# Summing the squares of the latent tokens on TensorE, and forming modulation columns one token tile later

## The chip, the cores and the metric

The kernel runs on one core of one Trainium2 chip. A core has five engines, each with its own instruction stream: TensorE (matrix products; PE in the profile, and PEld for its weight loads), VectorE (DVE), ScalarE (ACT), GpSimd (POOL) and SyncE (SP), which here only issues DMAs. They meet through semaphores alone. The metric is device time in microseconds (us), the median over several runs.

## The reference

Two layers of a transformer backbone on 512 latent tokens of width 1024, with 256 context tokens beside them. Each layer is `h += g1 * mixer(norm(h)); h += g2 * swiglu(norm(h))`; layer 0's mixer is a differential attention of 8 heads over latent and context tokens, layer 1's a short gated convolution. What bears on the change is the very first step, the modulated input of layer 0:

```python
mod = (silu(c) @ ada_w[i] + ada_b[i])                    # six vectors of 1024
sh1, sc1, g1, sh2, sc2, g2 = split(mod, 6)
a  = rmsnorm(x,   norm1[i]) * (1.0 + sc1)  + sh1         # latent tokens
ac = rmsnorm(ctx, norm1[i]) * (1.0 + csc1) + csh1        # context tokens
q, k, v = split(a @ w_qkv, ...)                          # and the same for ac
```

`rmsnorm` needs, for each token, the sum of its 1024 squares.

## The kernel before

Features lie on partitions, tokens along the free dimension. The 1024 features are 8 feature tiles (`KT`), the 512 latent tokens 4 token tiles (`LT`), the context tokens 2 more. Float32 products are made exact by splitting each operand in a high and a low part (`hi_w` and `lo_w` for weights, `aTh`/`aCh` and `aTl` for tokens) and adding three products. A plain float32 matmul, such as those of the statistics, leaves two records in the trace (two passes), so that 4 issued matmuls stand as x8.

The start of the program, all within the first 60 us, goes so. TensorE first runs 37 warm-up matmuls (`N_WARM`) on a tile of ones. `x_stats(LAT)` squares each of the 8 feature tiles of x on ScalarE (L268) and adds them up on VectorE (L270) in `ss`; then `stats` lets TensorE sum `ss` over the partitions, 4 matmuls with the data as stationary operand and 2 columns of ones as moving operand. VectorE scales the sums (`var_x`, L244), GpSimd takes the power -1/2 (`rs_x`, L247), VectorE makes diagonal matrices of the results (`dg_x`, L251), TensorE spreads them over all partitions (`x_bcast`) and ScalarE copies them to `bcs` (L276).

The modulation of a feature tile k takes three steps. `mod_dot(k)` multiplies the conditioning vectors with a 1 MB tile `ad` of the adaLN weights on TensorE, and ScalarE copies the result to `pas` (L311). `mod_cols(k)` turns it into columns by two small matmuls, and VectorE forms the shift (`mod`, L318) and the gain (`Gc`, L320). `mod_apply(k, i)` scales x on VectorE (L326), adds the shift and rounds to `aTh` on ScalarE (L327), and forms the rest `aTl` on VectorE (L328).

The loop over k then projects the first head: for each feature tile, three matmuls for each of the 4 latent token tiles into four PSUM banks, with the context tokens three steps behind. `mod_dot` runs two tiles ahead (`AHEAD`), and `mod_cols` of that tile ends the step. Weights of the first two heads come in units that a DMA loads (`raw_w`), ScalarE casts to `hi_w` (L180), and VectorE or GpSimd completes with `lo_w` (L181).

What sets the order: TensorE's stream is pinned to program order (`te.pin`, class `InOrder`, whose line 98 all its instructions bear). The streams of the other engines are ordered by the framework's scheduler when the program is built, and each engine then works its stream in order. Buffers come free by pool: the tag `sq` has 2 buffers, `ad` 4, `raw` 5, `pas` 2.

Of the kernel before, what the change touches and what calls it, by code (L numbers as in the profile page):

```python
# [14 lines left out]
# The order of issue in the attention. A head takes 24 positions, each with a quarter of the projections of  # L15
# one token tile of the next head (head 7: of one feature tile of the output projection); what else is issued,
# and at which position of its head, is listed here.
#   scores 0, scores 1, transpose 0, scores 2, transpose 1, scores 3, transpose 2, P V of tiles 0-1, transpose 3, P V of tiles 2-3
# [3 lines left out]
#   transposes of k tiles 2-3, q, k tiles 4-5 (head 0: k tiles 0-1, 2-3, q, k tiles 4-5)  # L22
TK = (2, 0, 4)
TK_OF = {0: (9, 9, 8, 10), 1: (0, 2, 4), 7: (3, 0, 3)}
#   transposes of k tiles 0-1 of the next head
TK_NEXT = 16
TK_NEXT_OF = {0: 12, 6: 15}
#   the weights of the head after the next, by feature tiles
W_AT = (16, 19, 22, 23, 23, 24, 26, 27)
W_AT_OF = {0: (11, 11, 15, 22, 22, 22, 25, 26)}  # L30
#   positions from the squares of a token tile to its rotation
LAG = 1
LAG_OF = {1: 0}
#   head 6: scale of the first six heads' outputs, its products, their exact parts
# [3 lines left out]
# halves of adaLN tiles per token tile of each head, per pair of gate and up tiles, per down tile  # L38
ADA_HEAD = (0, 2, 1, 1, 1, 1, 1, 1)
ADA_GATE, ADA_DOWN = 3, 3  # L40
# tile of the output projection before which the weights of the last two heads are staged
W67_AT = 6
# token tiles whose squares the activation engine also sums
ACC_TILES = (0, 1, 2, 3, 4)
# second parts of staged weights: 0 on the vector engine, 1 on the GpSimd engine
# [6 lines left out]
# the first head's projections: at which feature tile the second head's weights are staged, how many tiles the  # L52
# context lags behind the latent tokens, where its statistics and their broadcast come
W1_AT = (1, 2, 5, 5, 5, 8, 10, 10)
CTX_LAG, CTX_STATS, CTX_BCAST = 3, 1, 2
AHEAD = 2
N_WARM = 37
RAW_BUFS = 5
# pieces of the second half of the tokens after which the next norm's statistics and its products come
TURN = {8: (4, 7), 2: (1, 3)}  # L60
# feature tiles whose squares GpSimd sums for the norm after the attention
# [16 lines left out]
# columns of the packed parameters  # L78
# [9 lines left out]
class InOrder:  # L88
    """an engine; while pin is set its instructions are issued in program order"""
# [16 lines left out]
def kernel(  # L106
# [43 lines left out]
    mods = const.tile([P, 2, 6, KT], F32, name="mods")      # sh1 sc1 g1 sh2 sc2 g2  # L150
    part = const.tile([P, 2, 2, 6, KT], F32, name="part")   # halves of the dot products
    mod0 = const.tile([P, 2, 2, KT], F32, name="mod0")      # layer 0, latent and context: sh1 sc1
    Gc = const.tile([P, 5, KT], F32, name="Gc")             # norm gains times (1 + scale)
# [9 lines left out]
    # staging of the attention weights and the attention output: right stack  # L163
# [22 lines left out]
    def ada_half(i, half, pool, tag, bufs):  # L186
        """one half of the dot products of a tile of 128 columns of ada_w with silu(c)"""
        l, s, j = ada_list[i]
        raw = pool.tile([P, 512], F32, name=f"ada_{i}_{half}", tag=tag, bufs=bufs)
        nc.sync.dma_start(out=raw, in_=adaR[i, :, half * 512:(half + 1) * 512])  # L190
        ve.scalar_tensor_tensor(out=raw, in0=raw, scalar=1.0, in1=scrow[:, half * 512:(half + 1) * 512], op0=ALU.mult, op1=ALU.mult,  # L191
                                accum_out=part[:, half, l, s, j:j + 1])
# [10 lines left out]
    # =====================================================================  # L203
    # layer 0: modulated input, differential attention
    # =====================================================================
# [23 lines left out]
    # the tensor engine's clock rises while the first loads are under way  # L229
# [3 lines left out]
    # silu of the conditioning vectors  # L233
# [4 lines left out]
    def stats(sums, ntile, ps_stat, pool, nm):  # L238
        """rstd of the tokens from the columns of the partial sums, as diagonal matrices"""
        for t in range(ntile):  # L240
            for i, x in enumerate(sums):
                te.matmul(out=ps_stat[:, 2 * t:2 * t + 2], lhsT=x[:, t * P:(t + 1) * P], rhs=ones[:, 0:2], start=(i == 0), stop=(i == len(sums) - 1))
        var = pool.tile([P, 4], F32, name=f"var_{nm}", tag="var", bufs=1)
# [11 lines left out]
    def bcast(dgs, bc):  # L255
        """bc[t][:, q] = rstd of token q of tile t, the same on all partitions"""
# [3 lines left out]
    # 1 / rms of x and ctx, on all partitions  # L260
# [3 lines left out]
    def x_stats(s):  # L264
# [6 lines left out]
        return stats([ss[:, s]], n, pqkv0[5][:, SEQ - 16:], s0, f"x{n}")  # L271

# [27 lines left out]
    def mod_dot(k):  # L300
        """products of the conditioning vectors with the shift and scale columns of one feature tile"""
# [11 lines left out]
    def mod_cols(k):  # L313
        """shift and gain of one feature tile as columns, for the latent and the context tokens"""
# [7 lines left out]
    def mod_apply(k, i):  # L322
        """a = x rstd G + sh in two exact parts"""
# [11 lines left out]
    dgs = x_stats(LAT)  # L335
# [4 lines left out]
    for k in range(1, AHEAD):  # L340
        mod_dot(k)
        mod_cols(k)
    for k in range(KT + CTX_LAG):
# [5 lines left out]
        if k < KT:  # L349
            for t in range(LT):  # L350
                qkv_mm(pqkv0[t], t, k, W0[k])
        if j < KT:
            mod_dot(j)
        if k + 1 < KT:
# [9 lines left out]
        if j < KT:  # L364
            mod_cols(j)
# [6 lines left out]
    # gains of q and k folded into the rotary tables (q also takes 1 / sqrt(head dim))  # L372
# [9 lines left out]
    # lam = exp(q1 k1) - exp(q2 k2) + lam_init  # L382
# [30 lines left out]
    def qkv_post1(o, t, ps):  # L413
        """sums of squares of q and k of one token tile; v in two parts"""
# [21 lines left out]
    def qkv_post2(o, t, ps, st):  # L436
        """normalise and rotate q and k of one token tile"""
# [52 lines left out]
    def scores(o, t):  # L490
        """softmax of both maps for one tile of queries, combined: a = p0 - lam p1"""
# [58 lines left out]
    def o_rstd(b):  # L550
        """1 / sqrt(mean + eps) of the heads so far; 0 where the sum is beyond float32's range"""
# [12 lines left out]
    def o_apply(k):  # L564
        """o rstd subln (1 - lam_init), in place; rstd comes broadcast from DRAM"""
# [33 lines left out]
    def fill_qkv(nxt, W, t):  # L599
        """projections of one token tile of the next head, in quarters"""  # L600
# [14 lines left out]
    def fill_wo(n):  # L615
        """heads 0-5 of one feature tile of the output projection, in quarters"""
# [18 lines left out]
    def events(o, base):  # L635
        """what the attention of a head does, and from which position"""
# [75 lines left out]
    # =====================================================================  # L712
    # the rest: residual stream h (features on partitions), FFN and convolution
    # =====================================================================
# [21 lines left out]
    def residual(n, ps, gcol, nm, s=FULL):  # L736
        """h += gate * y for one feature tile; its squares go into the next norm's sum"""
# [17 lines left out]
    class Norm:  # L755
        """a = h rstd G + sh in two exact parts, by halves of the tokens"""
# [23 lines left out]
    def turn(last, norm):  # L780
        """the last products of a projection, by halves of the tokens, with the next norm's first half between them"""
# [14 lines left out]
    def group(U, norm, nm):  # L796
        """the first four units after a norm, the contraction outermost, by halves of the tokens"""
# [288 lines left out]
```

## Time and profile before

| | |
|---|---|
| time, median of 3 runs | 1342.76 us (1341.63 to 1345.31) |
| span of the profiled execution | 1343.2 us |
| TensorE busy | 1309.2 us (97%) |
| VectorE busy | 809.6 us (60%) |
| ScalarE busy | 503.9 us (38%) |
| GpSimd busy | 184.9 us (14%) |
| mean granted TensorE clock | 0.991 of full speed |

The profiled execution has no time of its own but its span, from the first to the last instruction; it lies 0.5 us above the median and inside the three runs. Busy shares are means over stages with different limits, so the start of the program is read by itself. A granted clock of 1.00 is 2.4 GHz and 0.50 is 1.2 GHz.

### The profile page before, as it was taken

The page shows a single profiled execution, that of the slowest core. Times are in us where ns is not written, and L with a number is a line of the kernel's source. Part 1 is how long each engine was busy: PE and PEld are TensorE (multiplying, and loading weights), DVE is VectorE, ACT ScalarE, POOL GpSimd, SP SyncE. Part 2 cuts the span into 40 slices and gives each one's busy share as a digit, 9 for nine tenths or more (in the row PEclk, how much of TensorE's full clock was granted, in tenths as well). Part 3 has the DMA queues.
Part 4 walks back from the last instruction along what each step waited for, and adds up shares of the span by engine and source line. Part 5 has one row for each costly group of instructions (what it writes and reads, how often), then busy time and mean ns, then how long its engine had stood idle before and what let it go on. Part 6 is the DMA issues. An engine that isn't in the chain of part 4 may idle for free.

```text
span 1343.2 us, 18899 instructions
## 1 busy us (share of the span) xinstructions
PE 1309.2 (97%) x7021; PEld 1130.8 (84%) x7021; DVE 809.6 (60%) x1598; ACT 503.9 (38%) x1125; POOL 184.9 (14%) x239
## 2 busy tenths in 40 slices
PE   8999999999999999899999999999999999999999
PEld 7889988998789888688888898888898888888887
DVE  5889888988968666665653366444664333333331
ACT  4677666776655321122221333222342212222120
POOL 0544444543302000000000020000100000000000
PEclk9999999999998999899999999999999999999999
DMA  9413333214333756677642333313323223322231
GB/s 350 160 41 112 94 95 90 71 59 146 106 118 103 224 197 196 198 241 224 203 134 67 110 109 109 97 55 96 118 72 121 81 72 109 125 94 85 70 105 40
DMA packets 72284, 164.59 MB, mean 123 GB/s; under 512 B 7784, under 2 KB 23424, under 8 KB 71168
## 3 DMA queue, kind: packets, MB, share of 16 engines
q1 hardware_dynamic: 72192, 163.38, 38.6%
q8 instruction: 55, 0.90, 0.3%
q14 instruction: 37, 0.30, 0.1%
HBM read 161.24 MB, written 2.11 MB: 122 GB/s over the span
## 4 chain that ended last, share of the span: by engine, by line
PE 74%; DVE 10%; DMA 8%; issue 3%; POOL 2%; ACT 2%; SPq 0%; POOLq 0%; DVEq 0%; ACTq 0%
PE pg L98 25%; PE pd L98 18%; PE pi L98 8%; PE pq L98 7%; DMA ada<-in_adaR_dram 6%; PE py L98 3%; PE s L98 3%; PE pw L98 3%; DVE ada L191 2%; PE pf_in L98 2%; PE pf_gu L98 2%; PE pv L98 1%; DMA xk<-in_xT_dram 1%; POOL st L432 1%; DMA raw_w<-in_wqkv_dram 1%
## 5 line engine op out<-in xcount | busy, mean ns | idle before, releaser
L727 ACT CAST sh_gu<-sr_gu 128x1024 fp32r<-128x1024 f32 x88 | 92.3, 1052 | 276.1 <-PE pg L98 147.9
L191 DVE SCALAR_TENSOR_TENSOR ada<-ada,scrow 128x512 f32<-128x512 f32 x160 | 110.6, 702 | 85.5 <-DMA ada<-in_adaR_dram 85.1
L728 DVE TENSOR_TENSOR sl_gu<-sr_gu,sh_gu 128x1024 fp32r<-128x1024 f32 x85 | 105.8, 1247 | 72.4 <-ACT sh_gu L727 65.3
L98 PE MATMUL pg<-xl_n0b,sh_gu 128*128 128x512 f32 x320 | 124.6, 389 | 0.0
L98 PE MATMUL pg<-xh_n0b,sh_gu 128*128 128x512 f32 x320 | 124.6, 389 | 0.0
L98 PE MATMUL pg<-xh_n1b,sh_gu 128*128 128x512 f32 x320 | 124.6, 389 | 0.0
L98 PE MATMUL pg<-xl_n1b,sh_gu 128*128 128x512 f32 x320 | 124.5, 389 | 0.0
L98 PE MATMUL pg<-xh_n1b,sl_gu 128*128 128x512 f32 x320 | 124.5, 389 | 0.0
L98 PE MATMUL pg<-xh_n0b,sl_gu 128*128 128x512 f32 x320 | 124.5, 389 | 0.0
L98 PE MATMUL pq<-hi_w,aTl 128*128 128x384 f32 (+1 forms) x336 | 108.5, 323 | 0.0
L98 PE MATMUL pq<-hi_w,aTh 128*128 128x384 f32 x224 | 77.3, 345 | 2.5 <-DVE qn L443 2.5
L839 DVE TENSOR_TENSOR sl<-sl,pg 128x512 f32<-128x512 f32 x40 | 27.4, 686 | 85.7 <-PE pg L98 85.7
L98 PE MATMUL pq<-lo_w,aTh 128*128 128x384 f32 x224 | 76.3, 341 | 0.0
L98 PEld LDWEIGHTS pg<-xh_n1b,sh_gu 128*128 128x128 f32 x320 | 60.1, 188 | 12.5
L98 PEld LDWEIGHTS pg<-xl_n0b,sh_gu 128*128 128x128 f32 x320 | 60.1, 188 | 12.5
L98 PEld LDWEIGHTS pg<-xh_n1b,sl_gu 128*128 128x128 f32 x320 | 60.1, 188 | 12.5
L98 PEld LDWEIGHTS pg<-xh_n0b,sh_gu 128*128 128x128 f32 x320 | 60.1, 188 | 12.5
L98 PEld LDWEIGHTS pg<-xl_n1b,sh_gu 128*128 128x128 f32 x320 | 60.1, 188 | 12.3
L98 PEld LDWEIGHTS pg<-xh_n0b,sl_gu 128*128 128x128 f32 x320 | 60.1, 188 | 12.3
L504 ACT ACTIVATE e<-s,l 128x768 f32<-128x768 f32 x64 | 58.0, 908 | 29.5 <-DVE l L502 18.4
L502 DVE TENSOR_REDUCE l<-s 128x1 f32<-128x768 f32 x64 | 60.0, 949 | 8.3 <-PE s L98 7.8
L98 PEld LDWEIGHTS pq<-hi_w,aTl 128*128 128x128 f32 x336 | 63.9, 190 | 0.0
(390 smaller groups left out, 3366.7 us busy)
## 6 DMA issues: line engine op xcount, KB each, us to landing
sr_gu<-in_wgu_dram SPq DMA_DIRECT2D x88, 512.0 KB, 3.9
ada<-in_adaR_dram SPq DMA_DIRECT2D x160, 256.0 KB, 3.2
raw_w<-in_wqkv_dram SPq DMA_DIRECT2D x64, 192.0 KB, 2.6
sr_in<-in_win_dram SPq DMA_DIRECT2D x24, 512.0 KB, 3.5
ad<-in_ada_dram SPq DMA_DIRECT2D x8, 1024.0 KB, 8.8
raw_wo<-in_wo_dram SPq DMA_DIRECT2D x16, 192.0 KB, 2.8
xk<-in_xT_dram SPq DMA_DIRECT2D x8, 256.0 KB, 5.3
h<-in_xT_dram SPq DMA_DIRECT2D x8, 256.0 KB, 6.1
```

Of the source, the lines that this page charges most:

```text
L98: ins = f(*args, **kw)
L191: ve.scalar_tensor_tensor(out=raw, in0=raw, scalar=1.0, in1=scrow[:, half * 512:(half + 1) * 512], op0=ALU.mult, op1=ALU.mult, accum_out=p ...
L432: nc.gpsimd.tensor_tensor(out=st[:, 4:4 + ns], in0=st[:, 0:ns], in1=nhalf[:, 0:ns], op=ALU.pow)
L502: ve.tensor_reduce(out=l[:, m:m + 1], in_=s[:, :, 0:384], axis=AX.XY, op=ALU.max, negate=True)
L504: ae.activation(out=em.rearrange("p (a b) -> p a b", a=2), in_=s[:, :, 0:384], func=AF.Exp, bias=l[:, m:m + 1], scale=1.0, accum_out=l[:, ...
L727: ae.copy(out=hi[:, :ncols], in_=raw[:, :ncols])
L728: lo_eng.tensor_tensor(out=lo[:, :ncols], in0=raw[:, :ncols], in1=fp(hi)[:, :ncols], op=ALU.subtract)
L839: ve.tensor_tensor(out=t[:, s], in0=t[:, s], in1=ps_u, op=ALU.mult)
```

## The change

Two edits, both in the first 60 us.

First, the squares of the latent tokens are no longer added up by VectorE. A new function squares each feature tile on ScalarE into a tile `sql` of the tag `sq`, and TensorE sums each of these tiles over the partitions at once, 4 matmuls for each of 8 feature tiles, all accumulated in the same 8 columns of PSUM. The context tokens keep the old way. Second, `mod_cols` of a feature tile moves behind the first token tile of the next projection, from the end of the step before.

```diff
...
+        return rstd_diag(ntile, ps_stat, pool, nm)
+
+    def rstd_diag(ntile, ps_stat, pool, nm):
...
+    def x_stats_lat():
+        ps_stat = pqkv0[5][:, SEQ - 16:]
+        for k in range(KT):
+            sq = s0.tile([P, TOK], F32, name=f"sql{k}", tag="sq", bufs=2)
+            ae.activation(out=sq[:, LAT], in_=xk[k][:, LAT], func=AF.Square)
+            for t in range(LT):
+                te.matmul(out=ps_stat[:, 2 * t:2 * t + 2], lhsT=sq[:, t * P:(t + 1) * P], rhs=ones[:, 0:2],
+                          start=(k == 0 and t == 0), stop=(k == KT - 1), skip_group_check=True)
+        return rstd_diag(LT, ps_stat, s0, "x4")
...
-    dgs = x_stats(LAT)
+    dgs = x_stats_lat()
     mod_dot(0)
     x_bcast(LAT, pqkv0[4], dgs)
     mod_cols(0)
     mod_apply(0, 0)
     for k in range(1, AHEAD):
         mod_dot(k)
-        mod_cols(k)
+    cols_of = AHEAD - 1
     for k in range(KT + CTX_LAG):
...
         if k < KT:
             for t in range(LT):
                 qkv_mm(pqkv0[t], t, k, W0[k])
+                if t == 0 and cols_of < KT:
+                    mod_cols(cols_of)
         if j < KT:
             mod_dot(j)
+            cols_of = j
+        else:
+            cols_of = KT
...
-        if j < KT:
-            mod_cols(j)
```

The order of instructions shows the first edit at the start of TensorE's stream. Before, the warm-up matmuls are followed by 4 matmuls on `ss`, the modulation product of feature tile 0 (`pa` from `ad`) and the spreading matmuls (`dg_x`):

```order
L98 MATMUL q_0_144<-ones 128x128 x37
L98 MATMUL q_5_149<-ones,ss 128x2 x4
L98 MATMUL pa_248<-ad_192,c_187 32x256 x8
L98 MATMUL q_4_148<-dg_x_0_240,ones 128x128
L98 MATMUL q_4_148<-dg_x_1_242,ones 128x128
```

Now there are eight such groups of 4, one for each feature tile, and they too stand behind the warm-up (five alike are left out):

```order
L98 MATMUL q_0_144<-ones 128x128 x37
L98 MATMUL q_5_149<-ones,sql_210 128x2 x4
L98 MATMUL q_5_149<-ones,sql_216 128x2 x4
...
L98 MATMUL q_5_149<-ones,sql_252 128x2 x4
L98 MATMUL pa_270<-ad_192,c_187 32x256 x8
L98 MATMUL q_4_148<-dg_x_0_262,ones 128x128
```

The sums thus grew from 4 matmuls to 32 in one stream, with nothing else between them; the seven additions into `ss` are gone from VectorE's stream.

The second edit shows on TensorE around the first projection. Before, the columns of feature tile 1 (the second `pa` from `pas`) stand ahead of the three matmuls of the first token tile (`q_0`, with weights `hi_w` and `lo_w` and tokens `aTh` and `aTl`):

```order
L98 MATMUL pa_248<-cst_sb,pas_257 128x2 x2
L98 MATMUL pa_271<-ad_200,c_187 32x256 x8
L98 MATMUL pa_271<-cst_sb,pas_280 128x2 x2
L98 MATMUL q_0_144<-hi_w_0_196,aTh_97 128x384
L98 MATMUL q_0_144<-lo_w_0_197,aTh_97 128x384
L98 MATMUL q_0_144<-hi_w_0_196,aTl_113 128x384
L98 MATMUL q_1_145<-hi_w_0_196,aTh_97 128x384
```

Now they stand behind them:

```order
L98 MATMUL pa_270<-cst_sb,pas_279 128x2 x2
L98 MATMUL pa_293<-ad_200,c_187 32x256 x8
L98 MATMUL q_0_144<-hi_w_0_196,aTh_97 128x384
L98 MATMUL q_0_144<-lo_w_0_197,aTh_97 128x384
L98 MATMUL q_0_144<-hi_w_0_196,aTl_113 128x384
L98 MATMUL pa_293<-cst_sb,pas_302 128x2 x2
L98 MATMUL q_1_145<-hi_w_0_196,aTh_97 128x384
```

So the first three projection matmuls no longer stand behind the columns; the columns are one token tile later at each step.

On ScalarE the scheduler moved a weight cast. Before, between the tokens of feature tiles 1 and 2 (`aTh_98`, `aTh_99`), two squares of context tokens (`sq`) stand ahead of the cast of the second weight unit (`hi_w_1_288`), and the copy `pas` of tile 2 is behind them:

```order
L327 ACTIVATE aTh_98<-xk_128,mod_70 128x512
L268 ACTIVATE sq_2_380<-xk_133 128x256
L268 ACTIVATE sq_2_383<-xk_134 128x256
L180 CAST hi_w_1_288<-raw_w_1_286 128x384
L180 CAST hi_w_2_326<-raw_w_2_324 128x384
L180 CAST hi_w_0_332<-raw_w_0_330 128x384
L311 COPY pas_315<-pa_306 128x256
L327 ACTIVATE aTh_99<-xk_129,mod_70 128x512
```

Now that cast (`hi_w_1_306`) comes right behind the tokens of tile 1, and the two squares behind it:

```order
L342 ACTIVATE aTh_98<-xk_128,mod_70 128x512
L180 CAST hi_w_1_306<-raw_w_1_304 128x384
L271 ACTIVATE sq_2_402<-xk_133 128x256
L271 ACTIVATE sq_2_405<-xk_134 128x256
L180 CAST hi_w_2_344<-raw_w_2_342 128x384
L180 CAST hi_w_0_350<-raw_w_0_348 128x384
L326 COPY pas_337<-pa_328 128x256
L342 ACTIVATE aTh_99<-xk_129,mod_70 128x512
```

One cast went ahead of two squares; the copy of tile 2's products (`pas_337`) still stands behind two squares and two casts. The streams of GpSimd and SyncE are the same as before, and all streams are the same behind the first head's projections.

## Rows read from the trace of the kernel before

**Rows 1.** The page's first lines: span; busy time, share and instructions of each engine.

```profile
span 1343.2 us, 18899 instructions
...
PE 1309.2 (97%) x7021; PEld 1130.8 (84%) x7021; DVE 809.6 (60%) x1598; ACT 503.9 (38%) x1125; POOL 184.9 (14%) x239
```

**Rows 2.** Busy time by stretch (instructions in brackets), granted TensorE clock, DMA share, GB/s.

```profile
12.52:13.67 1.15, 1.04 (x8) 0.97 (x8) 0.05 (x1) 0.00 (x0) 0.00 (x0) 1.00 1.04 419
...
14.00:18.00 4.00, 3.50 (x44) 2.33 (x44) 2.25 (x8) 1.47 (x3) 0.97 (x1) 1.00 1.03 377
...
18.15:19.90 1.75, 0.00 (x0) 0.00 (x0) 0.96 (x3) 1.62 (x5) 0.00 (x0) 1.00 1.09 318
...
21.00:24.00 3.00, 3.00 (x10) 2.65 (x9) 2.90 (x8) 2.44 (x6) 0.00 (x0) 0.50 1.02 413
...
30.00:40.00 10.00, 10.00 (x85) 7.92 (x81) 7.44 (x20) 5.06 (x11) 2.42 (x3) 1.00 1.01 373
...
40.00:50.00 10.00, 9.18 (x78) 7.28 (x77) 9.22 (x17) 5.82 (x13) 3.84 (x4) 1.00 0.36 114
```

**Rows 3.** Timeline, start to first modulation: start, length, engine, line, operation, count [idle before].

```profile
1.05 11.47 PE L98 MATMUL q<-ones 128*128 128x128 f32 x74 [1.05 <-DVE ones L144]
...
7.10 5.47 DVE L270 TENSOR_TENSOR ss<-ss,sq 128x512 f32<-128x512 f32 x7 [3.52 <-ACT sq L268]
...
11.12 0.63 ACT L268 ACTIVATE sq<-xk 128x512 f32<-128x512 f32 x1 [0.27 <-DMA xk<-in_xT_dram]
...
12.62 0.97 PEld L98 LDWEIGHTS q<-ones,ss 128*128 128x128 f32 x8 [0.30 <-DVE ss L270]
...
12.62 1.05 PE L98 MATMUL q<-ones,ss 128*128 128x2 f32 x8
...
14.11 0.62 PEld L98 LDWEIGHTS pa<-ad,c 128*32 128x32 f32 x16 [0.52 <-issue]
```

**Rows 4.** Timeline, from the token sums to the first projection.

```profile
13.96 1.01 POOL L247 TENSOR_TENSOR rs_x<-var_x,misc 128x4 f32<-128x4 f32 x1 [13.52 <-DVE var_x L244]
...
19.03 0.75 DVE L328 SCALAR_TENSOR_TENSOR aTl<-xk,mod,aTh 128x512 fp32r<-128x512 f32 x1 [0.79 <-ACT aTh L327]
...
19.52 0.35 ACT L311 COPY pas<-pa 128x256 f32<-128x256 f32 x1
...
19.92 0.61 PE L98 MATMUL pa<-cst_sb,pas 128*128 128x2 f32 x4 [1.77 <-ACT pas L311]
...
20.82 0.46 PE L98 MATMUL q<-hi_w,aTl 128*128 128x384 f32 x1
```

**Rows 5.** Groups by line, weight loads alone, 2.0 to 6.9 and 8.0 to 12.0 us.

```profile
L98 PEld LDWEIGHTS q<-ones 128*128 128x128 f32 x24 | 5.2, 333 | 0.0
...
L98 PEld LDWEIGHTS q<-ones 128*128 128x128 f32 x37 | 4.2, 192 | 0.0
```

**Rows 6.** Timeline, from the first projection to the second.

```profile
22.39 0.72 ACT L327 ACTIVATE aTh<-xk,mod 128x512 fp32r<-128x512 f32 x1 [0.24 <-DVE xk L326]
...
23.02 0.71 ACT L268 ACTIVATE sq<-xk 128x256 f32<-128x256 f32 x2
...
23.64 0.50 ACT L180 CAST hi_w<-raw_w 128x384 fp32r<-128x384 f32 x1
...
24.21 1.00 POOL L181 TENSOR_TENSOR lo_w<-raw_w,hi_w 128x384 fp32r<-128x384 f32 x1 [9.23 <-ACT hi_w L180]
...
26.40 0.61 PE L98 MATMUL pa<-cst_sb,pas 128*128 128x2 f32 x4 [0.64 <-ACT pas L311]
...
27.12 0.34 PE L98 MATMUL q<-lo_w,aTh 128*128 128x384 f32 x1
```

**Rows 7.** Waits of TensorE, 0 to 60 us (total, times, longest), and one timeline row.

```profile
PE pa L98 <- ACT pas L311: 3.2, 3, 1.8
...
PE pa L98 <- DMA ad<-in_ada_dram: 1.2, 3, 0.5
...
49.74 0.61 PE L98 MATMUL pa<-cst_sb,pas 128*128 128x2 f32 x4 [0.82 <-ACT pas L311]
```

## Prediction

> **What bounds the kernel now.** I read the page's first lines, then the start of the program by stretches, then the waits, then the timeline of the stretch that the change touches. The page says that TensorE is busy 97% of 1343.2 us [rows 1]: behind the start it works almost without a gap, so what the start loses or gains is lost or gained at the end, unless something in the start hides it. The stretches show where that could be [rows 2]: TensorE has no work at all from 18.15 to 19.90 us and is busy 10.00 of 10 us from 30 to 40, while the DMA engines are full in every stretch shown from 12 to 40 us (share 1.01 to 1.09). The waits name two things that hold up TensorE in these 60 us: the copy `pas` of ScalarE, 3.2 us in three places, and the adaLN tiles from DRAM, 1.2 us [rows 7].
>
> The timeline gives the chain to the first projection. The warm-up matmuls end at 1.05 + 11.47 = 12.52 us; VectorE's seven additions of squares run from 7.10 to 12.57; the 4 summing matmuls (8 records) start at 12.62 and end at 13.67 [rows 3]. Scaling, power, diagonals, spreading and modulation follow, one engine after the other: power from 13.96, and `aTl`, directly behind `aTh`, from 19.03 to 19.78 [rows 4]. TensorE then stands in front of the columns of tile 1, whose `pas` ScalarE copies only after `aTh`, until 19.92, and the third projection record, the first to need `aTl`, starts at 20.82 [rows 4].
>
> **Edit 1: the sums.** The additions that go away cost VectorE 5.47 us, but they end 0.05 us after the warm-up [rows 3], and TensorE works its stream in order. What can be gained is those 0.05 us; I count nothing. What comes instead: 8 feature tiles x 4 token tiles x 2 records = 64 records where 8 stood. Each has another 128x128 block of squares as its weights. The trace has the very form: eight weight loads span 0.97 us, the last one about 0.19 long (mean of one: 192 ns [rows 5]), so they start (0.97 - 0.19)/7 = 0.111 us apart, and the last ends 0.27 us after its load starts (13.67 against 12.62 + 0.97 - 0.19 = 13.40) [rows 3]. Since the records stand behind the warm-up, none of them can use the time in which x arrives. They end at 12.52 + 63 x 0.111 + 0.27 = 19.8 us in place of 13.67: **+6.1 us**. ScalarE doesn't make it longer: it has the first two squares done by then, and with two buffers each further square (0.63 us [rows 3]) waits for the records of the tile two before, 0.89 us of records apart, so the two engines just keep step. The near bound on the cheap side is the loads of 32 columns for the modulation, 16 in 0.62 us [rows 3], that is about 0.034 each: 64 of these end at 12.52 + 2.2 + 0.27 = 15.0, +1.3. I take the 0.111, since it is the same instruction with the same shapes.
>
> The Trainium skill speaks against such a price. In "TensorE: Matmul & The Clock Gate", section "Back-to-back issue gap", matmuls of 1 to 64 columns are listed at about 60 cycles, 25 ns at full clock, and it adds that this leaves the weight loads out. By its figure alone, as an estimate, 64 records would take 1.6 us and the sums end at 14.4. The rows have 111 ns, since every record brings its own weights.
>
> **The clock in that stretch.** The granted clock can be seen to fall after TensorE ran out of work: it is 0.50 (1.2 GHz) from 21 to 24 us, behind the empty 18.15 to 19.90 [rows 2]. For 7 us the new records do little but load weights: 2 columns stream behind each load, where a warm-up record streams 128. No row shows whether such a stretch keeps the clock at 2.4 GHz. Its price has a row: in the first microseconds, before the pace doubles, 24 weight loads of the warm-up stand in 4.9 us, 0.204 each, and later 37 in 4.0 us, 0.108 each [rows 5]. So each record at the lower level costs 0.096 us more. Bounds: 0, if the clock holds, and 64 x 0.096 = 6.1 if it fell at the start. In the rows the fall comes some 2 to 3 us after the work ran out, so it would fall inside the stretch; I take half of the records, 32 x 0.096 = **+3.1 us**.
>
> The same page (section "Part 1: The HAM clock gate (the "warmup" mystery)") calls the lower level the default, which activity releases. That agrees with the rows of the warm-up; what it would make of records like these isn't said there.
>
> **Edit 2: the columns.** At the first projection the two columns no longer stand in front. The third record can start when `aTl` is there, at 19.78 + 0.05 in the old times in place of 20.82 [rows 4]: **-1.0 us**. The copy `pas` then ends at about 19.4, a token tile before it is needed.
>
> To the second projection, the old way took from 20.82 to 27.12, its second record, the first to need `lo_w`, 6.3 us: slow matmuls, a wait for an adaLN tile, and 0.64 us for `pas` of tile 2 [rows 6]. The new way is another chain: the columns of tile 1 start 0.2 us behind the third record; from columns to the end of `aTh` it took 22.39 + 0.72 - 19.92 = 3.2 us [rows 4, 6]; the cast `hi_w`, now right behind it on ScalarE, 0.55; `lo_w` on GpSimd 1.0 and two handovers, 1.1 [rows 6]. Sum 5.1 us: **-1.2 us**. That chain holds at either clock, since twelve projection matmuls fit under it.
>
> On ScalarE, behind that cast, two squares (0.71 together), two casts (0.50 each [rows 6]) and only then `pas` of tile 2 (0.35 [rows 4]) stand in line: it ends 2.1 us behind the cast, where TensorE is through the first token tile of projection 1 about 1.5 us behind it. The wait moves there: **+0.6 us**.
>
> From then on I count nothing. The wait of 0.82 us at 49.74 [rows 7] goes, but VectorE is busy 9.22 of 10 us from 40 to 50 [rows 2], and the tokens of tile 7 need the columns that now come a token tile later. If VectorE had slack it would give 0.8; if the later columns delay its tokens once more it costs 0.8.
>
> Sum: +6.1 + 3.1 - 1.0 - 1.2 + 0.6 = +7.6 us. On the span of 1343.2 that is 1350.8; the span lies 0.5 above the median, so **1350.4 us**.
>
> **Rivals.** *The clock holds through the sums.* For it: the 4 summing matmuls and what follows up to 18 us ran at 1.00 [rows 2]. Against it: they stood among other work. Then the 3.1 us are missing: +4.5, 1347.3 us.
>
> *The loads hide it (not slower).* The DMA engines are full from 12 to 40 us [rows 2], so a loop that only waits for loads would take a later start without loss, and the wait of 0.82 us would still go: 1342.8 - 0.8 = 1342.0 us. It decides if TensorE waits for loads as long as the sums are late, 6 us, between 20 and 40. The rows give 1.2 us of such waits and a TensorE busy 10.00 of 10 [rows 2, 7]; against it.
>
> *The records are cheap.* If loads overlap as those of 32 columns do: +1.3 - 1.0 - 1.2 + 0.6 = -0.3, 1342.5 us, at most slightly faster. By the figure of the Trainium skill named above it would be 0.6 us less, an estimate. Against it: the eight records of rows 3.
>
> **How the numbers follow.** 0.3%, 4.0 us here, is about what a measurement of this kernel tells from no change. Chances: forecast 0.50, clock holds 0.36, loads hide it 0.07, cheap records 0.07. The forecast's own range is 1348.0 (little of the stretch at the lower clock) to 1353.4 (nearly all of it). The second case lies within 1.5 us of 1347.3, since the warm-up's end moves with the moment at which its pace doubles, and some 0.36 of it (0.13) is below 1346.8; with the two last cases that is 0.27 for no clear change or faster, of which 0.02 for faster. So slower 0.73, same 0.25, faster 0.02. The range goes from 1345.8 to 1353.4: it leaves out 0.14 for the last two cases and a little at both ends.
>
> **What would show it.** The summing records should run from 12.5 to between 19.8 and 23 us, about 0.11 apart, and 0.2 if the granted clock reads 0.50 before 20. The third projection record should be 5 to 8 us later than 20.82, directly behind `aTl`. The second projection should start behind a `lo_w` of GpSimd, and the columns of tile 2 wait about 0.6 us for `pas`. Near 50 us everything should be late by the same amount. I am wrong if the records stand much closer than 0.1 us, if the lateness shrinks between 25 and 50 us, or if the clock changes more after the sums than in them.

## The result, and the profile after

The changed kernel takes 1351.0 us (median of 6 runs, 1348.91 to 1352.9), the kernel before 1342.71 us (6 runs beside them, 1341.29 to 1345.31). The ratio is 1.0058, 95% interval 1.0042 to 1.0074: 7.8 us slower (5.6 to 9.9). The forecast was 1350.4 us and "slower".

The page's first lines after, for [rows 1]:

```profile
span 1350.2 us, 18996 instructions
...
PE 1321.0 (98%) x7077; PEld 1139.5 (84%) x7077; DVE 805.9 (60%) x1591; ACT 503.3 (37%) x1125; POOL 184.9 (14%) x239
```

TensorE is 11.8 us busier with 56 records more; VectorE has 3.7 us less to do, and the time doesn't fall with it. Now the stretches of the start (columns as in [rows 2]: length, busy time of PE, PEld, DVE, ACT and POOL, granted clock, DMA share, GB/s):

```profile
10.00:14.00 4.00, 4.00 (x39) 4.00 (x37) 0.00 (x0) 1.60 (x3) 0.00 (x0) 1.00 1.05 427
14.00:15.00 1.00, 1.00 (x8) 1.00 (x7) 0.00 (x0) 0.63 (x2) 0.00 (x0) 0.61 1.00 410
15.00:24.50 9.50, 9.43 (x51) 8.07 (x52) 1.52 (x6) 2.32 (x5) 1.28 (x1) 0.50 0.93 321
...
32.00:34.50 2.50, 1.62 (x8) 1.21 (x9) 2.40 (x5) 1.73 (x6) 1.17 (x1) 1.00 0.10 26
34.50:38.20 3.70, 3.70 (x21) 2.67 (x24) 2.78 (x7) 1.54 (x3) 0.00 (x0) 0.54 0.81 248
```

TensorE is all but full from 10 to 24.5 us (4.00 of 4.00, 1.00 of 1.00 and 9.43 of 9.50 us), yet the granted clock goes from 1.00 to 0.50 while it works, near 14.2 us. After it came back, it fell once more, to 0.54 from 34.5 to 38.2, behind a thin stretch (1.62 of 2.50 us). The timeline to the first projection, for [rows 3, 4]:

```profile
10.80 10.60 PE L98 MATMUL q<-ones,sql 128*128 128x2 f32 x64
11.84 0.63 ACT L282 ACTIVATE sql<-xk 128x512 f32<-128x512 f32 x1 [4.96 <-PE q L98]
...
21.33 1.93 PE L98 MATMUL pa<-ad,c 128*32 128x256 f32 x16
...
23.33 1.68 PE L98 MATMUL q<-dg_x,ones 128*128 128x128 f32 x8
...
27.54 0.75 DVE L343 SCALAR_TENSOR_TENSOR aTl<-xk,mod,aTh 128x512 fp32r<-128x512 f32 x1 [0.79 <-ACT aTh L342]
...
28.34 0.45 PE L98 MATMUL q<-hi_w,aTl 128*128 128x384 f32 x1 [0.17 <-DVE aTl L343]
...
28.62 0.50 PE L98 MATMUL pa<-cst_sb,pas 128*128 128x2 f32 x4
```

The 64 summing records take 10.60 us where 8 took 1.05, 0.166 apart on the mean. ScalarE's squares wait for TensorE and not the other way round (4.96 us before the third). The third projection record, at 28.34, stands directly behind `aTl` and ahead of the columns, as the second edit wants, but 7.5 us later than in [rows 4]. From there to the third projection, for [rows 6]:

```profile
30.90 0.72 ACT L342 ACTIVATE aTh<-xk,mod 128x512 fp32r<-128x512 f32 x1 [0.24 <-DVE xk L341]
31.52 0.49 ACT L180 CAST hi_w<-raw_w 128x384 fp32r<-128x384 f32 x1
...
32.10 1.17 POOL L181 TENSOR_TENSOR lo_w<-raw_w,hi_w 128x384 fp32r<-128x384 f32 x1 [9.14 <-ACT hi_w L180]
...
33.31 0.44 PE L98 MATMUL q<-lo_w,aTh 128*128 128x384 f32 x1 [0.81 <-POOL lo_w L181]
33.36 0.36 ACT L326 COPY pas<-pa 128x256 f32<-128x256 f32 x1
...
33.78 0.61 PE L98 MATMUL pa<-cst_sb,pas 128*128 128x2 f32 x4
...
35.29 0.52 PE L98 MATMUL q<-lo_w,aTh 128*128 128x384 f32 x1
...
39.00 0.43 PE L98 MATMUL q<-hi_w,aTh 128*128 128x384 f32 x1
```

`aTh`, `hi_w`, `lo_w` and the second record of the second projection follow each other; `pas` is ready before TensorE gets to the columns. The record at 35.29 is 0.52 long: this is the second fall of the clock. The waits of TensorE in 60 us, for [rows 7]:

```profile
PE q L98 <- ACT aTh L342: 1.5, 2, 1.2
...
PE q L98 <- POOL lo_w L181: 0.8, 1, 0.8
```

The waits for `pas` and for the adaLN tiles are gone; what is waited for is the chain of one feature tile to the next.

To attribute time, a landmark early in the program serves better than the end: the first record into `pq`, where the next head's projection begins and all streams are the same again. Before it stands at 58.43 us, after at 67.42, 9.0 later. The spans differ by 7.0 only, because the profiled execution of before took 1284.8 us from that mark to its end, that of after 1282.8, and seven of the ten below 1280.9 to 1282.0. A time holds 1.9 us around the span (1352.12 us for the span of 1350.2), so that execution of before took about 1345.1 us, among the longest of the six, and not 0.5 more than the median as the prediction had it; since the 7.6 us were added to the median in the end, the forecast stands. The landmark, then, says where the time went in one execution, and the ratio how much it is.

### The profile page after: what moved, and what is told of

Same layout as the page of the kernel before. It is cut to its first block, busy times and chain, and to the rows that moved or that the text cites. A ratio compares the mean times of both kernels' runs of the same rounds, so it can differ in the third digit from the quotient of the medians.

```text
span 1350.2 us, 18996 instructions
## 1 busy us (share of the span) xinstructions
PE 1321.0 (98%) x7077; PEld 1139.5 (84%) x7077; DVE 805.9 (60%) x1591; ACT 503.3 (37%) x1125; POOL 184.9 (14%) x239
## 4 chain that ended last, share of the span: by engine, by line
PE 76%; DVE 10%; DMA 7%; issue 3%; POOL 2%; ACT 2%; POOLq 0%; SPq 0%; DVEq 0%; ACTq 0%
PE pg L98 25%; PE pd L98 18%; PE pi L98 8%; PE pq L98 7%; DMA ada<-in_adaR_dram 5%; PE py L98 3%; PE s L98 3%; PE pw L98 2%; DVE ada L191 2%; PE q L98 2%; PE pf_in L98 2%; PE pf_gu L98 2%; PE pv L98 1%; POOL st L450 1%; POOL lo_w L181 1%
## 5 line engine op out<-in xcount | busy, mean ns | idle before, releaser
L98 PEld LDWEIGHTS pg<-xh_n0b,sh_gu 128*128 128x128 f32 x320 | 60.1, 188 | 12.6
```

Of the source, the lines that this page charges most:

```text
L98: ins = f(*args, **kw)
```

## Experiments

Ten kernels, all of which compute the whole reference. "Sums end" is where the last summing record ends; "mark" is the start of the first record into `pq`, and its distance to the 58.43 of before. The kernel before drifted from 1342.7 to 1344.4 us between the chips used, so ratios to the runs beside them are compared.

| kernel | time, us (runs) | ratio to before, 95% | sums end | mark |
|---|---|---|---|---|
| before | 1342.71 (6) | | 13.67 | 58.43 |
| after | 1351.0 (6) | 1.0058, 1.0042 to 1.0074 | 21.4 | +9.0 |
| e1_sums_alone | 1352.43 (6) | 1.0074, 1.0053 to 1.0094 | 21.4 | +7.9 |
| e2_columns_alone | 1343.38 (11) | 0.9992, 0.9982 to 1.0003 | | -0.5 |
| e3_warmup_between | 1363.65 (4) | 1.0144, 1.0130 to 1.0159 | 31.3 | +21.4 |
| e4_short_warmup | 1349.11 (5) | 1.0036, 1.0022 to 1.0050 | 18.0 | +5.9 |
| e5_short_warmup_wide | 1342.1 (11) | 0.9987, 0.9972 to 1.0001 | 14.1 | 0.0 |
| e6_lo_on_vector | 1351.45 (6) | 1.0056, 1.0038 to 1.0074 | 21.5 | +9.1 |
| e7_wide_sums | 1348.75 (6) | 1.0040, 1.0027 to 1.0052 | 19.3 | +7.0 |
| e8_wide_old_columns | 1344.58 (12) | 0.9998, 0.9986 to 1.0009 | 13.5 | +2.9 |
| e9_columns_and_loads | 1347.96 (8) | 1.0033, 1.0021 to 1.0045 | | +5.2 |
| e10_wide_and_loads | 1350.23 (6) | 1.0043, 1.0029 to 1.0057 | 14.3 | +5.1 |

### The two edits apart

`e1_sums_alone` keeps the sums and puts the columns back to the end of the step before:

```diff
         mod_dot(k)
-    cols_of = AHEAD - 1
+        mod_cols(k)
...
-                if t == 0 and cols_of < KT:
-                    mod_cols(cols_of)
...
+        if j < KT:
+            mod_cols(j)
```

> Edit 1 alone: the 64 summing records, with the columns where they were before. Theory (the loss is in the sums, the columns' new place gains 1.6 us): sums as in the changed kernel, from about 10.8 to 21.4 us, and the time 1.6 us above the changed kernel's, 1352.6 us. Rival A (the columns' new place costs as well, by the wait for lo_w and the second fall of the clock at 34.7 us that the changed kernel shows): below the changed kernel, 1348 to 1350 us.

Measured: 1352.43 us, +9.9 us by the ratio (7.1 to 12.6); the forecast's number was met, and the sums alone are the whole loss. The six runs scatter from 1349.93 to 1358.88 us, and the profiled one is the shortest. TensorE's timeline in `e1_sums_alone`:

```profile
10.88 10.53 PE L98 MATMUL q<-ones,sql 128*128 128x2 f32 x64
...
27.91 0.91 PE L98 MATMUL pa<-cst_sb,pas 128*128 128x2 f32 x4 [1.46 <-ACT pas L326]
...
29.47 0.52 PE L98 MATMUL q<-hi_w,aTl 128*128 128x384 f32 x1
...
34.09 0.61 PE L98 MATMUL pa<-cst_sb,pas 128*128 128x2 f32 x4 [0.79 <-ACT pas L326]
...
34.81 0.34 PE L98 MATMUL q<-lo_w,aTh 128*128 128x384 f32 x1
```

The sums take the same 10.5 us and end at the same 21.4, so this run and after can be laid on each other. The third projection record comes at 29.47 against 28.34 (1.1 later without edit 2), the second projection's second record at 34.81 against 33.31 (1.5 later). Part of this is the clock, which is at 0.51 from 28 to 31.5 us here. At the mark the order is the other way round: after stands 1.1 us behind `e1_sums_alone` (the table), so these two traces don't show a gain by edit 2 that lasts.

`e2_columns_alone` keeps only the second edit:

```diff
-    dgs = x_stats_lat()
+    dgs = x_stats(LAT)
```

> Edit 2 alone: VectorE adds the squares as before, the columns come behind the first token tile. Theory: 1.6 us gained, 1341.1 us, the first projection's third record at about 19.9 us in place of 20.8. Rival A: nothing gained or up to 2 us lost, 1342.7 to 1344.7 us, with TensorE waiting for lo_w at the second projection.

Measured: 0.9992, that is -1.1 us (-2.4 to +0.4). The medians themselves are level, so this missed the expected time, though the interval still holds the 1.6 us. TensorE in `e2_columns_alone`:

```profile
19.78 0.44 PE L98 MATMUL q<-hi_w,aTl 128*128 128x384 f32 x1 [0.17 <-DVE aTl L343]
...
23.94 1.07 PE L98 MATMUL pa<-ad,c 128*32 128x256 f32 x16 [1.71 <-DMA ad<-in_ada_dram]
```

The third record comes 1.04 us earlier than in [rows 4], as worked out, but then TensorE waits 1.71 us for the third adaLN tile, which isn't there before 23.9 us whatever TensorE does. In the kernel before that matmul started at 24.68 with 0.52 us of waiting. So the load takes part of the early start, 0.74 us of lead being left there. At the context statistics (`ones,ss`) the lead is 1.26 us (28.86 against 30.12), also because the clock has no fall here, and at the mark 0.5: the rest goes between these two, of which more below.

### The clock in the sums

`e4_short_warmup` shortens the warm-up, so that the sums start when x arrives:

```diff
-N_WARM = 37
+N_WARM = 10
```

> The changed kernel with 10 warm-up matmuls in place of 37, so that the sums start as soon as the first squares are there. Theory: nothing then brings the clock up, so the records stand about 0.21 us apart, 1.7 us for each feature tile, and end at about 5.4 + 8 x 1.7 = 19 us, 2.4 us earlier than in the changed kernel: 1348.5 us. Rival B (the records cost what they cost, wherever they stand and whatever the clock): end near 12.5 + 7 = 19.5 or later and time 1350 us; rival C (only the place behind the warm-up costs, not the clock): sums done at 13 us and the time at or below 1342 us.

`e5_short_warmup_wide` is the same, but each summing matmul has 128 columns of ones in place of 2. The streams of all other engines are the same as in `e4_short_warmup`, instruction for instruction:

```diff
...
-        ps_stat = pqkv0[5][:, SEQ - 16:]
+        ps_stat = pqkv0[5]
...
-                te.matmul(out=ps_stat[:, 2 * t:2 * t + 2], lhsT=sq[:, t * P:(t + 1) * P], rhs=ones[:, 0:2],
+                te.matmul(out=ps_stat[:, P * t:P * t + P], lhsT=sq[:, t * P:(t + 1) * P], rhs=ones,
```

> As the kernel with 10 warm-up matmuls, but each summing matmul streams 128 columns of ones in place of 2, the same number of records with the same weights; the sums stand in 128 equal columns. Theory: they act as the warm-up, the clock is up by about 8 us and the records keep up with the squares, so that the sums end at 13 to 14 us, at or a little before the 13.7 of the kernel before, and edit 2's 1.6 us come on top: 1341 us. Rival B (wide records cost more): sums done at 19 us or later, 1348 us or more.

Measured on one chip: 1349.11 and 1342.1 us, both near what was expected. But `e4_short_warmup` got there another way: its clock did come up, its first eight records take 1.05 us as in [rows 3], and it fell again near 8 us. First `e4_short_warmup`, TensorE's timeline and its stretches:

```profile
5.39 1.05 PE L98 MATMUL q<-ones,sql 128*128 128x2 f32 x8 [0.16 <-ACT sql L282]
6.90 11.10 PE L98 MATMUL q<-ones,sql 128*128 128x2 f32 x56 [0.46 <-ACT sql L282]
```

```profile
4.60:8.00 3.40, 2.79 (x24) 2.51 (x22) 0.00 (x0) 1.99 (x4) 0.00 (x0) 1.00 0.98 289
8.00:18.00 10.00, 10.00 (x52) 9.98 (x55) 0.00 (x0) 3.55 (x6) 0.00 (x0) 0.50 1.04 395
```

Then `e5_short_warmup_wide`, the same two views:

```profile
5.54 8.59 PE L98 MATMUL q<-ones,sql 128*128 128x128 f32 x64
...
23.87 1.07 PE L98 MATMUL pa<-ad,c 128*32 128x256 f32 x16 [1.13 <-DMA ad<-in_ada_dram]
```

```profile
5.54:14.10 8.56, 8.49 (x66) 7.84 (x65) 0.00 (x0) 4.41 (x7) 0.00 (x0) 1.00 1.02 373
14.10:25.00 10.90, 7.77 (x78) 5.35 (x77) 7.36 (x21) 6.67 (x17) 1.27 (x2) 1.00 0.98 351
```

Records that stream 64 times as many columns are done sooner: 0.134 us apart (they wait a little for squares too) against 0.198. With 2 columns the clock is at 0.50 from 8 us on; with 128 it stays at 1.00 through the sums and on to 40 us and beyond. These kernels differ in the moving columns alone, so it is these that lose or keep the clock here, and that is worth 7.0 us by the medians and 6.6 by the ratios, 0.0049 apart. The waits of 0.16 and 0.46 us ahead of the fall in `e4_short_warmup` aren't what decides it, since the changed kernel loses the clock in its sums with no such wait, and `e7_wide_sums` below keeps it. Over the runs whose sums began with the clock up, it fell within narrow sums in the changed kernel, `e1_sums_alone`, `e4_short_warmup` and `e6_lo_on_vector`, and within wide ones in none of `e5_short_warmup_wide`, `e7_wide_sums`, `e8_wide_old_columns` and `e10_wide_and_loads`. Of the cost 3.9 us lie in the sums in the traces (18.00 against 14.13) and the rest behind them: the narrow kernel is at 0.50 to 21.7 us and at 0.51 from 25 to 32, the wide one, at 1.00, waits 1.13 us at 23.87 for the load that `e2_columns_alone` waits for.

`e7_wide_sums` makes the sums wide, with the 37 warm-up matmuls ahead of them as in the change (the diff is that of `e5_short_warmup_wide`, from the changed kernel; its source differs from that of `e5_short_warmup_wide` in the 27 more warm-up matmuls alone):

> The changed kernel, all 37 warm-up matmuls ahead of the sums, but each summing matmul streams 128 columns of ones in place of 2 (same 64 records, same weights). ScalarE's and VectorE's order differ too: context squares come earlier. Theory (half of the loss is the clock, half the records that stand behind the warm-up): granted clock 1.00 to the end of the sums, records about 0.11 to 0.13 us apart, sums done at 18 to 20 us in place of 21.4, time 1347 to 1348 us, 3 us below the changed kernel and 4.5 above the one before. Rival B (the fall of the clock costs nothing in the end, since later stages take it back): 1351 us. Rival D (the clock is the whole loss): 1343 us.

Measured: 1348.75, +5.4 us by the ratio (3.6 to 7.0), expected were 1347 to 1348. TensorE's timeline and stretches in `e7_wide_sums`:

```profile
11.50 7.78 PE L98 MATMUL q<-ones,sql 128*128 128x128 f32 x64
```

```profile
11.50:19.20 7.70, 7.70 (x66) 7.43 (x64) 0.56 (x1) 4.14 (x8) 0.00 (x0) 1.00 0.95 364
19.20:25.00 5.80, 3.61 (x46) 2.28 (x45) 4.45 (x14) 4.92 (x13) 1.64 (x2) 1.00 0.86 300
25.00:35.00 10.00, 9.20 (x47) 7.17 (x48) 5.51 (x12) 2.13 (x5) 0.37 (x1) 0.66 1.02 407
```

64 records in 7.78 us, 0.122 apart, at a clock of 1.00: the place behind the warm-up costs 5.6 us (19.28 against 13.67) with no clock in it. Against `e5_short_warmup_wide` (0.9987) the 27 warm-up matmuls ahead of the same sums cost 7.1 us by the ratios. The clock falls only behind the sums, in the thin stretch to 25 us, as it does in [rows 2].

`e3_warmup_between` was meant to hold the clock by putting warm-up matmuls between the sums: 5 ahead and 4 behind the sums of each feature tile.

```diff
-N_WARM = 37
+N_WARM = 5
...
+            for i in range(4):
+                te.matmul(out=pqkv0[0][:, 0:P], lhsT=ones, rhs=ones, start=True, stop=True)
```

> The changed kernel with the same 37 warm-up matmuls, but only 5 of them ahead of the sums and 4 behind each feature tile's sums, so that the 64 records never stand alone. Theory (the clock fell because the sums stood alone): granted clock 1.00 up to the end of the sums, records 0.11 us apart, sums done at 18 to 19.6 us, time about 1347 us. Rival B (the clock falls or the records are slow whatever stands between them): sums still done at 21 us or later, time 1350 to 1351 us.

Measured: 1363.65 us, 16 us above the expectation, a clear miss. TensorE's timeline in `e3_warmup_between`:

```profile
5.50 1.87 PE L98 MATMUL q<-ones,sql 128*128 128x2 f32 x8 [1.95 <-ACT sql L282]
7.23 2.05 PE L98 MATMUL q<-ones 128*128 128x128 f32 x8
...
29.56 1.71 PE L98 MATMUL q<-ones,sql 128*128 128x2 f32 x8
...
37.22 1.07 PE L98 MATMUL pa<-ad,c 128*32 128x256 f32 x16
```

The first of eight pairs of 8 sums and 8 warm-up records and the start of the last stand here. From 5.50 to 29.56 us it is 24.06 us for seven pairs, 0.215 a record: the pace of the lower level (0.204 in [rows 5]), with no gap from 5.5 to 37 us. The clock column reads 1.00 all this while, since it shows no level before its first change; the pace of known records tells the level, the column doesn't. Only at 37.22 do the 16 records of the modulation take 1.07 us, as at full clock. So it isolates nothing of the change; its loss of 20 us holds the low pace and the 64 warm-up records between the sums together.

### The chain of the second edit

`e6_lo_on_vector` gives `lo_w` of the second weight unit, for which TensorE waits 0.81 us, to VectorE:

```diff
-LO_QKV0 = (0, 1, 0, 0, 1, 1, 1, 1)
+LO_QKV0 = (0, 0, 0, 0, 1, 1, 1, 1)
```

> The changed kernel with the second weight unit's low part made by VectorE in place of GpSimd; nothing else differs. Theory: TensorE's wait in front of the second projection's second record (0.81 us for lo_w) goes down by 0.5 us, and if the second fall of the clock at 34.7 us hangs on that gap, its 1.5 us go too: 1349.0 to 1350.5 us. Rival A2 (that wait is covered by the later columns): no change, 1351 us.

Measured: 1.0056 against 1.0058 of the change: nothing is gained, which was the number of rival A2. One of TensorE's stretches in `e6_lo_on_vector`:

```profile
21.50:32.90 11.40, 10.99 (x59) 8.00 (x60) 6.07 (x18) 4.82 (x12) 1.27 (x1) 0.50 0.81 313
```

The wait for `lo_w` is gone from the timeline, and so is the second fall of the clock behind it, but here the clock stays low to 32.9 us and slows the first projection. One fall around the first two projections is paid in either case.

`e8_wide_old_columns` is `e5_short_warmup_wide` with the columns at their old place (the diff of `e1_sums_alone`), to price edit 2 where the sums cost nothing:

> The kernel with 10 warm-up matmuls and 128-column sums, with the columns back in their old place: edit 2's worth where the clock stays up. Theory: 1.6 us above the kernel with the new place (1342.1 us): 1343.7 us. Rival E (what edit 2 gains at the first projection is lost again at the second, where TensorE waits for the next adaLN tile): equal within 0.5 us, 1342 us.

Measured: 0.9998 against 0.9987 for `e5_short_warmup_wide` (another chip). The difference, 1.5 us, is near what edit 2 was worth by its terms (1.6), but the intervals overlap and the runs aren't of one chip, so it isn't shown. The traces give it another ground as well: the clock is at 0.50 from 26 to 32.5 us in `e8_wide_old_columns` and at 1.00 in `e5_short_warmup_wide`.

The last two try to remove the load that `e2_columns_alone` waits for: the second weight unit and the third adaLN tile are issued ahead of the context tokens. `e9_columns_and_loads` is `e2_columns_alone` and `e10_wide_and_loads` is `e5_short_warmup_wide` with this:

```diff
     ad_load(1)
+    W0.append(qkv_unit(0, 1, engines[LO_QKV0[1]]))
+    ad_load(2)
     load_x(CON)
```

> Edit 2 alone, and the second weight unit and the third adaLN tile loaded ahead of the context tokens in place of behind them. Theory (with edit 2 alone TensorE waits 1.7 us at 23.9 us for that adaLN tile, so what it gains at the first projection goes into this wait): the wait goes, the second projection starts 1 to 2 us earlier, time 1341 to 1342 us where edit 2 alone has 1343.4. Rival F (the later context tokens hold up the context statistics and give it back): 1343 us or more.

> The kernel with 10 warm-up matmuls, 128-column sums and edit 2, with the same change of the loads. Theory: 1 to 2 us below that kernel's 1342.1: 1340.5 to 1341 us, below both kernels. Rival F: 1342 us or more.

Measured: 1347.96 and 1350.23 us, slower than without it by 5.5 and 7.5 us (1.0033 against 0.9992, 1.0043 against 0.9987), a miss in both. TensorE in `e9_columns_and_loads`, timeline and two stretches:

```profile
23.70 1.07 PE L98 MATMUL pa<-ad,c 128*32 128x256 f32 x16
...
30.72 1.07 PE L98 MATMUL pa<-ad,c 128*32 128x256 f32 x16 [3.12 <-DMA ad<-in_ada_dram]
```

```profile
15.00:21.30 6.30, 5.75 (x35) 3.89 (x32) 3.23 (x9) 2.35 (x5) 0.58 (x2) 0.50 1.03 385
...
32.00:38.50 6.50, 6.50 (x32) 5.60 (x35) 3.41 (x8) 1.53 (x4) 2.58 (x3) 0.50 0.98 394
```

and the timeline in `e10_wide_and_loads`, whose clock from 32 to 38.5 us is 0.51:

```profile
30.09 1.07 PE L98 MATMUL pa<-ad,c 128*32 128x256 f32 x16 [1.84 <-DMA ad<-in_ada_dram]
```

The third adaLN tile is no longer waited for, but the fourth is, 3.12 and 1.84 us, and behind it the clock is down for 6.5 us. The DMA engines were full already [rows 2], so what one tile gained the next lost. That the gap brought the clock down is likely, but no run takes the one without the other. Nor is this all of the loss: the clock is also at 0.50 ahead of that wait, from 15 to 21.3 us in `e9_columns_and_loads`, whose profiled run is the longest of its eight, and at 0.51 from 21.3 to 24.6 in `e10_wide_and_loads`. Whether the moved loads brought these falls isn't shown. Rival F's wait stands in one place only: 0.47 us for `ss` at 31.63 us in `e10_wide_and_loads`.

## Why the prediction was right, point by point

**The sums are dear because each record loads its weights.** Right. The forecast had 7.3 us for 64 records at full clock and 3.1 for the clock, 10.4; the trace has 10.60. `e7_wide_sums`, without the clock's fall, has 7.78. The figure of the Trainium skill ("TensorE: Matmul & The Clock Gate", section "Back-to-back issue gap") that the prediction weighed, 25 ns without the weight loads, isn't met in any run: the mean is 0.122 us at full clock and 0.166 with the fall in it. The sums end only 7.7 us later and not 9.2, since the warm-up of this execution let them start at 10.80 and not at 12.52; the moment at which its pace doubles differs from execution to execution, and the prediction had charged that start in both kernels alike.

**The clock falls within the sums.** Right, and shown by `e4_short_warmup` against `e5_short_warmup_wide` and by the changed kernel against `e7_wide_sums`. The row that the prediction went by had a fall behind an empty stretch; that a full one loses the clock as well was a guess, and so was half of the records, which came close: it fell 3.4 us into the stretch, and 10.60 - 7.3 = 3.3 us were lost against 3.1 predicted. It also slowed what followed up to 24.5 us, which no term had: the 16 modulation records of tile 0 took 1.93 us, those of tile 1, at full clock again, 1.07 in the same trace, and the 8 spreading ones 1.68 against 1.16 in `e5_short_warmup_wide`.

**The first projection, -1.0.** Right for the old sums: 1.04 in `e2_columns_alone`, with the clock at 1.00 on both sides. Behind the new sums it is 1.1 between `e1_sums_alone` and after, which have the same start, but 0.66 of that is the low clock in `e1_sums_alone`, where the way from the columns to the third record took 1.56 us (27.91 to 29.47) and not the 0.90 of [rows 4]. Against the kernel before it hardly shows (sums +7.7, third record +7.5), because the slow spreading (1.68 against 1.16) and a slower power on GpSimd (1.28 against the 1.01 of [rows 4]) took most of it.

**To the second projection, -1.2 and +0.6.** Partly wrong. The chain was as described, columns, `aTh`, `hi_w`, `lo_w` of GpSimd, 4.7 us from 28.62 to 33.31 where 4.9 was worked out for it (5.1 with the 0.2 ahead of the columns). But against `e1_sums_alone` it brings 0.4 more and not 1.2, for without edit 2 that stretch took 5.3 us (29.47 to 34.81) in place of the 6.3 of [rows 4, 6]; the 0.52 us of waiting for an adaLN tile in these 6.3 is not there any more, since the loads had 7 us to come in. The mis-sized term is the old way's length, which was read where a load was late and the clock was down for longer. The wait of 0.6 for `pas` didn't come: `pas` was done 1.7 us behind the cast and not 2.1, and TensorE, behind a `lo_w` of 1.17 us, reached the columns 1.8 us behind it and not 1.5, when `pas` had been done for 0.06 us.

**Nothing from then on.** Wrong in its working, small in its sum. The third projection starts at 39.00, 7.85 us later than in the kernel before (31.15), and 1.6 of that were added between the second projection (+6.2) and it. What added them is the fall from 34.5 to 38.2 us: seven records of that step are 0.49 to 0.52 long and some 0.32 apart, in place of 0.34 and 0.17, and the modulation behind them takes 1.58 us and not 1.07, 1.6 in all. The kernel before has such a fall too, in its first projection (0.50 from 21 to 24 us, [rows 2]). It wasn't made but moved, from the first projection, which now runs at 1.00, to the second. That the wait for `lo_w` brought it on is supported by `e6_lo_on_vector`, where wait and second fall are both absent, but the first projection is slow there, so the cause isn't isolated.

From the third projection to the mark another 1.1 us are added. Of these half a microsecond is one pair of columns, which the old order has ahead of that projection and the new one within it. The rest shows from the context statistics to the mark, over the same 216 records of TensorE, first before, then after, and in the two waits of after there:

```profile
30.12:58.43 28.31, 27.35 (x216) 23.17 (x213) 23.55 (x54) 16.75 (x51) 10.81 (x12) 1.00 0.64 223
```

```profile
38.53:67.42 28.89, 27.90 (x216) 22.77 (x213) 23.90 (x53) 16.32 (x51) 11.22 (x12) 1.00 0.56 194
```

```profile
53.04 0.44 PE L98 MATMUL q<-hi_w,aTh 128*128 128x384 f32 x1 [0.34 <-ACT aTh L342]
...
62.74 0.44 PE L98 MATMUL q<-hi_w,aTl 128*128 128x384 f32 x1 [0.36 <-DVE aTl L343]
```

The wait for `pas` of [rows 7] is gone, and TensorE waits for tokens of the sixth and of the last feature tile in its place. This stretch takes 28.2 to 28.5 us in the three kernels with the old place of the columns (before, `e1_sums_alone`, `e8_wide_old_columns`) and 28.9 to 29.2 in six with the new one (after, `e2_columns_alone`, `e4_short_warmup` to `e7_wide_sums`), all at a clock of 1.00. So edit 2 costs some 0.7 us there, which eats a good part of what it gains at the start. The prediction had named this case, later columns that delay the tokens once more, at 0.8, and counted nothing.

**The sum.** That 7.6 and 7.8 lie so close is in part luck. By the terms the lateness should have been 9.2 us at the end of the sums, 8.2 at the third record, 7.0 at the second projection and 7.6 from then on; in the trace it was 7.7, 7.5, 6.2 and at last 9.0. The sums were put 1.5 us too high; behind the second projection 2.8 us came on top where the terms had 0.6. The two errors offset each other, and everything late by the same amount, as the prediction wanted it near 50 us, isn't what the trace has.

**The rivals.** That the clock holds is out (`e5_short_warmup_wide` and `e7_wide_sums` show what it would have been: +5.4 by `e7_wide_sums`, against the 4.5 of that rival). That loads hide the loss is out for the change, as TensorE didn't wait for a single adaLN tile; but a late load takes part of the gain in `e2_columns_alone`, and a kernel with edit 2 alone isn't measurably faster. Cheap records are out.

So of the 7.8 us by the ratio, 5.4 are the place of 64 weight-loading records behind the warm-up, by `e7_wide_sums`, in which ScalarE's and VectorE's order differs too, and 2.4 are left for the clock that fell in them, the second with intervals that overlap (1.0027 to 1.0052 against 1.0042 to 1.0074). What edit 2 gives back isn't shown: by the ratios 1 to 2 us (0.0016 between `e1_sums_alone` and after, 0.0008 in `e2_columns_alone`), none of them beyond its interval, and by the marks 0.5 us gained in `e2_columns_alone` and 1.1 lost between `e1_sums_alone` and after. The fastest version, `e5_short_warmup_wide`, is level with the kernel before (0.9987, 0.9972 to 1.0001): sums that start while x arrives and keep the clock end 0.5 us after VectorE's way there and 0.2 before it in `e8_wide_old_columns`, and neither kernel is measurably faster, so even done well the first edit won nothing here.

What stays open: what decides whether a thin stretch like that before 34.5 us brings the clock down. The kernel before, `e1_sums_alone`, `e7_wide_sums` and `e8_wide_old_columns` have such a fall between 20 and 35 us, `e2_columns_alone` and `e5_short_warmup_wide` have none with gaps of 1.1 to 1.7 us.

## What to carry to other kernels

Before moving a reduction onto TensorE, ask whether TensorE has time at that point: count the weight loads, not the columns (here, at full clock, 0.12 us a record with 128 columns and 0.11 with 2), and look at what else the engine's stream has to finish first. A long run of matmuls with few moving columns can lose the clock while the engine is never idle, and more columns can then be faster; compare the pace of known records in the trace. A gain in front of a full DMA queue is worth only as much as the next load is early, and loads moved up push others back. Follow a moved instruction to the end of its loop: columns that came later saved 1.0 us at the first step and cost 0.7 at the last ones.

## What the runs showed that was not expected

The clock fell in the middle of a stretch in which TensorE's busy share was full (5.00 of 5.00 us from 15 to 20, 0.50), and two kernels that differ in nothing but 2 or 128 moving columns kept or lost it. In `e3_warmup_between` alternating groups of 8 wide and 8 narrow records left TensorE at the lower pace for 27 us without a gap. Columns that come a token tile later were paid for at the far end of the loop, in every one of six traces. The section "Part 1: The HAM clock gate (the "warmup" mystery)" of the Trainium skill's page "TensorE: Matmul & The Clock Gate" has activity release the higher level; here an engine that the profile shows as busy without pause from 5.5 us on didn't get it until 37 us.
